# A two-layer diffusion transformer on one core: low halves of weights added by DMA, three more seven-product block pairs, and modulation work moved between tiles

## The chip, the cores and the metric

The kernel runs on one core of one Trainium2 chip, as a single launch. The core has five engines with queues of their own: TensorE (PE: matrix products into PSUM; its weight loads are listed apart as PEld), VectorE (DVE), ScalarE (ACT), GpSimd (POOL) and SyncE (SP), whose queue issues DMA transfers here. Within one queue the order is fixed when the program is built; between queues the work is ordered by semaphores. The metric is the time of one execution on the device in microseconds, as the median of several executions.

## The reference

Two layers, batch 1, 256 latent tokens and 256 context tokens, model width 1024, everything in float32. Each layer is a feed-forward block (SwiGLU, hidden width 2816), a mixer (a short convolution in layer 0, grouped-query attention in layer 1) and a second feed-forward block. Each of them is preceded by an RMS norm with a shift and a scale, and its result is gated; shifts, scales and gates ("modulation") come from a matrix product with the conditioning vector. The context stream is dropped after the attention. Cut to what matters:

```python
for i in range(DEPTH):                       # DEPTH = 2
    mod  = (silu(c)     @ mod_w[i] + mod_b[i]).reshape(bsz, 3, 3, 1, D_MODEL)
    modc = (silu(c_ctx) @ mod_w[i] + mod_b[i]).reshape(3, 3, D_MODEL)
    lat = lat + 0.5 * mod[:, 0, 2] * _swiglu(_modulate(lat, ...), ffn_w13[i, 0], ffn_w2[i, 0])
    cx  = cx  + 0.5 * modc[0, 2]   * _swiglu(_modulate(cx, ...),  ffn_w13[i, 0], ffn_w2[i, 0])
    h, hc = _modulate(lat, ...), _modulate(cx, ...)
    y, yc = _short_conv_mixer(...) if i == 0 else _gqa_mixer(...)
    lat = lat + mod[:, 1, 2] * y
    # context: the same, then its second feed-forward block, in layer 0 alone
    lat = lat + 0.5 * mod[:, 2, 2] * _swiglu(_modulate(lat, ...), ffn_w13[i, 1], ffn_w2[i, 1])

def _swiglu(h, w13, w2):
    gte, up = jnp.split(h @ w13, 2, axis=-1)
    return (silu(gte) * up) @ w2
```

## The kernel before

**Split products.** Activations stand transposed, features on partitions, the 512 tokens (latent, then context) along the free axis. [...] A product is three matmuls: high by high, high by low, low by high (`mm3`, lines 131 to 133; the third one, L133, is the one that reads the weights' low part). Splitting is `split` (L107): ScalarE writes the high part (L108), VectorE subtracts it from the source (L109).

**Loading weights.** `load_raw` (L102) issues a load on SP's queue into one of 8 buffers `wr`. The halves go to rings of 4 buffers `wh` and `wl` (`half`, L111), 1024 columns each. `load_w` (L117) loads and splits one block of 2048 columns.

**The feed-forward block** (`ffn`, L754). The 22 blocks of the hidden width go in thirds of 8, 7 and 7 (`THIRDS`). In each third the first product (`w13`) makes the gated hidden values of the third's blocks, then `project` (L569) multiplies them by the second weights (`w2a`, `w2b`), eight output tiles m = 0 to 7, and adds the result to the residual `x`. Both streams are computed together in layer 0 and in the first feed-forward block of layer 1 (`tot == T2`, 512 columns); the last one has the latent stream alone.

For 512 columns most blocks of the first product are done by `Pair` (L675): a two-by-two scheme with seven products instead of eight (7 products x 4 x 3 = 84 matmuls of 256 columns, against 48 matmuls of 512 for a block as it stands). It needs sums of the weights' quarters (`sums`, L696: VectorE), splits of them (`keep`), and a separate split of the quarter A22 into buffers `w4h` and `w4l` (L706 to L709, a ring of 2). A22 is used in a pair's last product (`four`, L749), which is run inside the following pair. The sums of the activations' quarters (T1 to T4) are made once for each block of the network. `AS_IS` (L25) lists the blocks of a first third that are done as they stand: 3 to 7 in the first feed-forward block, beside the blocks 0 to 2 of a start that is written out by hand.

**The second product** (`project`). Tiles m = 0, 1, 2 (two of them where no pair is left over) run side by side, with the last two products of the last pair between them; then one tile after the other, the last two split by stream if the projection ends the block (`late`). `ws2` (L847) loads and splits the weights of one tile; `get` (L586) asks for tiles up to two ahead. `finish` (L547) adds the gated result to `x`, and `tail` makes the sums of squares for the next norm.

**Modulation.** Apart from two chunks made by TensorE at the start, every modulation value is a dot product on VectorE: a unit (`mod_unit`, L167, tile `junk`) takes one 128x1024 tile of weights, and two units per stream pair share one load. The units are spread over the program by `tick(n)` (L210): each call owes n more units. `gate_of` (L233) makes sure that the whole chunk of a gate is done, and multiplies it by 0.5 where the reference does; `lazy_gate` (L865) calls it when the first tile needs it.

**Order.** The start is written out by hand (`FIRST_STEPS`), as is the attention; everywhere else a scheduler orders each engine's queue from the program's order and its own estimates. The convolution is in lines 1064 to 1101, the attention's output projection in line 1372; both output projections take their weights through `by_pairs` (L1103), two tiles in a pair of buffers.

Of the kernel before, what the change touches and what calls it, by code (L numbers as in the profile page):

```python
# [9 lines left out]
F32 = mybir.dt.float32  # L10
F32R = mybir.dt.float32r
BF16 = mybir.dt.bfloat16
AF = mybir.ActivationFunctionType
# [8 lines left out]
NM = 22  # L22
THIRDS = (8, 7, 7)

AS_IS = {(0, 0): range(3, 8), (0, 1): (), (1, 0): ()}  # L25

EARLY = 4
HEADS = 8
# [19 lines left out]
def hybrid_kernel(ctx: ExitStack, tc: tile.TileContext, a: dict, out: bass.AP):  # L48
# [58 lines left out]
    def split(hi, lo, src):  # L107
        nc.scalar.activation(out=hi, in_=src, func=AF.Copy)  # L108
        return nc.vector.tensor_tensor(out=lo, in0=src, in1=hi.bitcast(F32), op=ALU.subtract)  # L109

    def half():  # L111

        return tuple(
            wp.tile([P, 1024], F32R, name=nm(t), tag=t, bufs=4) for t in ("wh", "wl")
        )

    def load_w(src, n=2048, fine=False):  # L117
        raw = [load_raw(src[:, c : c + 1024]) for c in range(0, n, 1024)]
        hs = [half() for _ in raw]
        step = 512 if fine else 1024  # L120
        for c in range(0, n, step):
            hi, lo = hs[c // 1024]
            d = slice(c % 1024, c % 1024 + min(step, n - c))
            split(hi[:, d], lo[:, d], raw[c // 1024][:, d])
        return lambda o, w=P: tuple(t[:, o % 1024 : o % 1024 + w] for t in hs[o // 1024])

    def mm3(ps, w, m, first, last, more=False):
# [39 lines left out]
    def mod_unit(l, ch, pair, raw, j, v):  # L167

        mt = mod_tile(l, ch)
        kt = pair * 2 + j  # L170
        col = ch * KT + kt
        junk = mp.tile([P, D], BF16, name=nm("junk"), tag="junk", bufs=1)
        nc.vector.tensor_tensor_reduce(  # L173
            out=junk,
            in0=raw[j],
            in1=scbc[:, v, :],
            scale=1.0,
            scalar=modb[:, l, col : col + 1],
            op0=ALU.mult,
            op1=ALU.add,  # L180
            accum_out=mt[:, kt, v : v + 1],
        )
        done[l, ch] += 1
# [47 lines left out]
        return t  # L231

    def gate_of(l, j):  # L233
        m = mod_ready(l, 3 * j + 2)
        if j == 1:
            return m
        t = const.tile([P, KT, 2], F32, name=f"G{l}{j}", tag=f"G{l}{j}")
        nv = 1 if (l, j) == (1, 2) else 2
        nc.vector.tensor_scalar(
            out=t[:, :, :nv], in0=m[:, :, :nv], scalar1=0.5, scalar2=None, op0=ALU.mult  # L240
        )
        return t


    accs = {}
# [299 lines left out]
        return tail  # L545

    def finish(m, ps, c0, c1, gate, tail, wide=False):  # L547
        g = gate()
        for s in range(2):
            for o in [s * S - c0] if not wide else range(0, T2 if s == 0 else 0, S):  # L550
                if not c0 <= s * S < c1:
                    continue
                nc.vector.scalar_tensor_tensor(  # L553
                    out=x[:, m, s * S : s * S + S],
                    in0=ps[:, o : o + S],
                    scalar=g[:, m, s : s + 1],
                    in1=x[:, m, s * S : s * S + S],
                    op0=ALU.mult,
                    op1=ALU.add,
                )  # L560
        if tail:
            tail(m, c0, c1)
# [6 lines left out]
    def project(ws, src, nk, gate, tail, tot, late, ev, between=()):  # L569

        def products(ps, w, ks, c0, c1, wide=True):
            ms = [src(k, c0, c1) for k in ks]
            if wide and len(ms[0]) == 3:
                return mm_wide(ps, [w(k) for k in ks], ms, ks[0] == 0, ks[-1] == nk - 1)
            for k, m in zip(ks, ms):  # L580
                mm3(ps[:, : c1 - c0], w(k), m[:2], k == 0, k == nk - 1)

        nf = 3 if between else 2
        ahead = {}

        def get(m):  # L586
            for i in range(m, min(m + 3, KT)):
                if i not in ahead:
                    ahead[i] = ws(i)
            return ahead[m]  # L590

        w2 = [get(m) for m in range(nf)]
        p2 = [psum("py") for _ in range(nf)]
        cut = nk - 2 if between else nk - 1
        for i in range(nf):
            products(p2[i], w2[i], range(cut), 0, tot)
            if i < len(between):
                between[i]()
        if between:
            for i in range(nf):  # L600
                products(p2[i], w2[i], (nk - 2,), 0, tot)
        for i in range(nf):
            products(p2[i], w2[i], (nk - 1,), 0, tot)
            finish(i, p2[i], 0, tot, gate, tail, len(src(0, 0, tot)) == 3)
            tick(ev)

        for m in range(nf, KT - late):
            if tail and tot == S and m == KT - 2:
                ready()
            w = get(m)  # L610
            ps = psum("py")
            wide = len(src(0, 0, tot)) == 3 and m < KT - 1
            products(ps, w, range(nk), 0, tot, wide)
            finish(m, ps, 0, tot, gate, tail, wide)
            tick(ev)
        if late:

            wl = [get(m) for m in (6, 7)]
            if tail:
                ready()  # L620
            for s in range(2):
# [53 lines left out]
    class Pair:  # L675
# [4 lines left out]


        def __init__(self, src, h):
            self.h, self.w = h, {}
            self.raw = [load_raw(src[:, c : c + 1024]) for c in (0, 1024)]
            ts = half()
            for i, key in enumerate(("A11", "A12")):
                self.w[key] = [t[:, i * T2 : i * T2 + T2] for t in ts]
                split(*self.w[key], self.raw[i][:, T2:])
# [7 lines left out]
        def sums(self, n):  # L696
# [9 lines left out]
            self.w["A22"] = [  # L706
                wp.tile([P, T2], F32R, name=nm(t), tag=t, bufs=2) for t in ("w4h", "w4l")
            ]
            split(*self.w["A22"], r2[:, :T2])  # L709
            v = lambda t: t.rearrange("p (a c) -> p a c", a=2)  # L710
            tt(  # L711
                out=v(r2), in0=v(r2), in1=s2.unsqueeze(1).to_broadcast([P, 2, T2]),
# [38 lines left out]
            nc.vector.tensor_tensor(out=self.gm, in0=self.sg, in1=self.u, op=ALU.mult)  # L751
            split(g[0], g[1], self.gm)

    def ffn(l, b, h, tot, gate, tail, gs=(), ev=1.5, z=None):  # L754
        gs = list(gs)
        i0 = 0
        for t, n in enumerate(THIRDS):
            between = ()
            if tot == T2:
# [21 lines left out]
                prev = None  # L781
                for i in range(len(gs), n):
                    if t == 0 and not heads and i in AS_IS[l, b]:
                        w = load_w(a["w13"][l, b, i])
                        pp = psum("pg"), psum("pu")
                        if prev:
                            prev.seven()
# [8 lines left out]
                        w13_mm(pp, w, h, range(4, KT), 0, T2)  # L796
                        gs.append(new_pair("g"))
                        w13_post(pp, gs[-1], 0, T2)
                        tick(4)
                        continue  # L800
                    if heads:
                        pr = heads.pop(0)
# [44 lines left out]
            def ws2(m):  # L847
# [1 line left out]
                o = (m % 2) * n * P  # L849
                raw = load_raw(src[:, o : o + n * P], n * P)  # L850
                hi, lo = half()
                split(hi[:, : n * P], lo[:, : n * P], raw[:, : n * P])
                return lambda k: (hi[:, k * P : k * P + P], lo[:, k * P : k * P + P])

            cur = gs
# [2 lines left out]
                ws2,  # L858
                (lambda k, c0, c1: cur[k]) if tot == S
                else lambda k, c0, c1: (cur[k][0][:, c0:c1], cur[k][1][:, c0:c1]), n,  # L860
                gate, tail if end else None, tot, 2 if end and tot == T2 else 0, ev, between,
            )
            gs = []

    def lazy_gate(l, j):  # L865
        box = []

        def get():
            if not box:
                box.append(gate_of(l, j))  # L870
            return box[0]

        return get


    h = Plain()
# [170 lines left out]
    for i in range(3):  # L1047
        gs0.append(new_pair("g"))
        w13_post(pps[i], gs0[i], 0, T2)

    with tc.issue_after(rows["last"]):
        convk = cload("convk", [P, 3, KT])
        qg = cload("qg", [P, 1])
# [3 lines left out]


    hn = Plain()
    ffn(0, 0, h, T2, lazy_gate(0, 0), tail_norm(0, 1, hn), gs0, 2)  # L1060
    h = hn

    zs = []
    for m in range(KT):
# [4 lines left out]
        for c0, c1 in ((0, S), (S, T2)) if m == 0 else ((0, T2),):  # L1069
# [11 lines left out]
        u = tp.tile([P, T2], F32, name=nm("u"), tag="gm", bufs=3)  # L1081
        nc.vector.tensor_tensor(out=u, in0=xv, in1=pc, op=ALU.mult)
        d = tp.tile([P, T2], F32, name=nm("d"), tag="gm", bufs=3)
        nc.vector.tensor_scalar(
            out=d, in0=u, scalar1=convk[:, 1, m : m + 1], scalar2=None, op0=ALU.mult
        )
        u2 = u.rearrange("p (s t) -> p s t", s=2)
        d2 = d.rearrange("p (s t) -> p s t", s=2)
        nc.vector.scalar_tensor_tensor(
# [13 lines left out]
    def by_pairs(key, box=None):  # L1103
        box = box or {}

        def ws(m):
            if m // 2 not in box:
                box[m // 2] = load_w(a[key][m // 2])
            w = box[m // 2]
            return lambda k: w(k * 256 + (m % 2) * P)  # L1110

# [2 lines left out]
    hn = Blocks()  # L1114
    project(
        by_pairs("cw_out"), lambda k, c0, c1: (zs[k][0][:, c0:c1], zs[k][1][:, c0:c1]), KT,
        lazy_gate(0, 1), tail_norm(0, 2, hn), T2, 2, 1.5,
    )
    h = hn
    hn = Blocks()  # L1120
    ffn(0, 1, h, T2, lazy_gate(0, 2), tail_norm(1, 0, hn), (), 1.7)
    h = hn


    hn = Plain()
    ffn(1, 0, h, T2, lazy_gate(1, 0), tail_norm(1, 1, hn), (), 1.5)
    h = hn
    ap = ctx.enter_context(tc.tile_pool(name="ap", bufs=2))

# [210 lines left out]
    with tc.manual_schedule(engines={e.engine for e in (nc.tensor, nc.vector, nc.scalar, nc.gpsimd)}):  # L1340
# [29 lines left out]
    hn, hz = Beside(), Early()  # L1370
    roomy.append(True)
    project(
        by_pairs("wo", wos), lambda k, c0, c1: aos[k], KT, lazy_gate(1, 1), tail_early(1, 2, hn, hz), S, 0, 0,
    )
    ffn(
        1, 1, hn, S, lazy_gate(1, 2),
        lambda m, c0, c1: nc.sync.dma_start(out[m], x[:, m, :S]), z=hz,
    )

# [79 lines left out]
```

## Time and profile before

| what | value |
|---|---|
| median of 3 runs | 1569.32 us (1567.46 to 1571.04) |
| the profiled execution's own time | 1571.47 us |
| its span in the trace | 1569.7 us |
| granted TensorE clock | 0.998 |
| loads from SP and ACT (queues q1, q10) | 247 MB |
| low parts by VectorE, 128x1024 / 128x896 / 128x512 (A22) | 250 / 64 / 54 instructions |
| modulation units on VectorE | 224 |

The span is the stretch between the first and the last instruction that the profiler recorded. An engine's busy time is the time during which at least one of its instructions ran; a PE that is busy all the time can still be waiting a little, since the ends of its matmuls are modelled and overlap. The distance between the starts of two matmuls, and the list of waits, tell more than the busy share. In a row of a group, the last part (after the bar) is the busy time, the mean duration of one in ns, and the idle time of the engine ahead of them with its releaser.

### The profile page before, as it was taken

What the parts mean: (1) busy time and instruction counts of PE and PEld (TensorE: products, weight loads), DVE (VectorE), ACT (ScalarE), POOL (GpSimd) and SP (SyncE); (2) the same over time, 40 slices, a digit from 0 to 9 for tenths busy, and PEclk for the clock granted to TensorE, in tenths of its full rate; (3) what the DMA queues carried; (4) which work ended last, traced back from release to release, by engine and by line L of the source; (5) the groups of instructions that cost most, each with busy time, mean ns of one, the idle gap of its engine ahead of it and who ended that gap; (6) DMA issues with size and microseconds to landing.
All of it is one profiled execution on the core that took longest, in us unless ns stands there. A gap on an engine that the chain in (4) does not pass through costs nothing.

```text
span 1569.7 us, 25671 instructions
## 1 busy us (share of the span) xinstructions
PE 1557.7 (99%) x10210; PEld 1422.0 (91%) x10210; DVE 1333.4 (85%) x2129; ACT 733.8 (47%) x1213; POOL 25.4 (2%) x20
## 2 busy tenths in 40 slices
PE   9999999999999999999999999999999999999999
PEld 7888998999888899989899899999899889898888
DVE  5998789899997698978989989969978887887676
ACT  5622452545322365435345465435345445674553
POOL 0000000000000000000000000000000002300000
PEclk9999999999999999999999999999999999999999
DMA  9675246355565323542533614533733853366562
GB/s 373 224 237 180 89 132 187 107 173 159 194 209 166 114 75 108 177 146 87 189 126 117 196 41 135 187 108 118 239 112 114 265 154 106 123 207 221 171 199 75
DMA packets 72120, 248.80 MB, mean 159 GB/s; under 512 B 9024, under 2 KB 10816, under 8 KB 72000
## 3 DMA queue, kind: packets, MB, share of 16 engines
q1 hardware_dynamic: 69408, 245.40, 48.0%
q10 hardware_dynamic: 2592, 1.76, 0.4%
q8 instruction: 80, 1.31, 0.3%
q14 instruction: 40, 0.33, 0.1%
HBM read 244.77 MB, written 1.05 MB: 157 GB/s over the span
## 4 chain that ended last, share of the span: by engine, by line
PE 88%; DVE 6%; DMA 2%; ACT 2%; issue 1%; POOL 0%; POOLq 0%; SPq 0%; ACTq 0%; DVEq 0%
PE py L131 8%; PE py L132 8%; PE py L133 8%; PE p L131 6%; PE p L133 6%; PE p L132 6%; PE q L133 5%; PE q L131 4%; PE q L132 4%; PE py L139 2%; PE pu L139 2%; PE pg L139 2%; PE pg L132 1%; PE pg L133 1%; DMA wr<-in_w 1%; PE pu L132 1%
## 5 line engine op out<-in xcount | busy, mean ns | idle before, releaser
L108 ACT ACTIVATE wh<-wr 128x1024 fp32r<-128x1024 f32 (+2 forms) x442 | 393.7, 916 | 361.9 <-PE py L132 119.6
L109 DVE TENSOR_TENSOR wl<-wr,wh 128x1024 fp32r<-128x1024 f32 (+2 forms) x442 | 454.5, 1048 | 95.1 <-ACT wh L108 76.2
L173 DVE CUSTOM_DVE_ANT_0 junk<-wr,scbc,modb 128x1024 bf16<-128x1024 f32 x218 | 279.4, 1282 | 15.2 <-DMA wr<-in_modT 13.1
L131 PE MATMUL py<-gh,wh 128*128 128x512 f32 (+1 forms) x570 | 214.7, 377 | 0.0
L132 PE MATMUL py<-gl,wh 128*128 128x512 f32 (+1 forms) x570 | 214.0, 375 | 0.0
L133 PE MATMUL py<-gh,wl 128*128 128x512 f32 (+1 forms) x570 | 213.9, 375 | 0.0
L133 PEld LDWEIGHTS py<-gh,wl 128*128 128x128 f32 x570 | 108.3, 190 | 19.0
L131 PEld LDWEIGHTS py<-gh,wh 128*128 128x128 f32 x570 | 108.5, 190 | 18.4
L132 PEld LDWEIGHTS py<-gl,wh 128*128 128x128 f32 x570 | 108.5, 190 | 18.2
L131 PE MATMUL p<-th,wh 128*128 128x256 f32 x432 | 122.3, 283 | 0.0
L132 PE MATMUL p<-tl,wh 128*128 128x256 f32 x432 | 122.3, 283 | 0.0
L133 PE MATMUL p<-th,wl 128*128 128x256 f32 x432 | 122.2, 283 | 0.0
L553 DVE SCALAR_TENSOR_TENSOR x<-py,G,x 128x256 f32<-128x256 f32 x189 | 83.5, 479 | 36.3 <-PE py L133 25.1
L133 PE MATMUL q<-bh,wl 128*128 128x256 f32 x320 | 91.5, 286 | 0.1
L131 PE MATMUL q<-bh,wh 128*128 128x256 f32 x320 | 90.9, 284 | 0.4 <-ACT wh L108 0.4
L132 PE MATMUL q<-bl,wh 128*128 128x256 f32 x320 | 90.5, 283 | 0.0
L132 PEld LDWEIGHTS p<-tl,wh 128*128 128x128 f32 x432 | 82.8, 192 | 0.3
L131 PEld LDWEIGHTS p<-th,wh 128*128 128x128 f32 x432 | 82.8, 192 | 0.3
L133 PEld LDWEIGHTS p<-th,wl 128*128 128x128 f32 x432 | 82.8, 192 | 0.0
L108 ACT ACTIVATE w4h<-wr 128x512 fp32r<-128x512 f32 x54 | 33.8, 625 | 75.1 <-DMA wr<-in_w 56.9
L108 ACT ACTIVATE gh<-gm 128x512 fp32r<-128x512 f32 x66 | 41.6, 630 | 56.0 <-DVE gm L751 53.8
L711 DVE TENSOR_TENSOR wr<-wr,wr 128x1024 f32<-128x1024 f32 x54 | 66.0, 1222 | 0.7
(303 smaller groups left out, 3946.3 us busy)
## 6 DMA issues: line engine op xcount, KB each, us to landing
wr<-in_w SPq DMA_DIRECT2D x176, 512.0 KB, 4.5
wr<-in_modT SPq DMA_DIRECT2D x122, 512.0 KB, 4.5
wr<-in_w2b SPq DMA_DIRECT2D x64, 448.0 KB, 3.9
wr<-in_w2a SPq DMA_DIRECT2D x32, 512.0 KB, 4.7
pm<-in_mod SPq DMA_DIRECT2D x16, 512.0 KB, 10.2
wr<-in_cw_cx SPq DMA_DIRECT2D x16, 512.0 KB, 4.7
wr<-in_cw_b SPq DMA_DIRECT2D x8, 512.0 KB, 4.4
wr<-in_cw_out SPq DMA_DIRECT2D x8, 512.0 KB, 3.9
```

Of the source, the lines that this page charges most:

```text
L108: nc.scalar.activation(out=hi, in_=src, func=AF.Copy)
L109: return nc.vector.tensor_tensor(out=lo, in0=src, in1=hi.bitcast(F32), op=ALU.subtract)
L131: nc.tensor.matmul(ps, wh, mh, start=first, stop=False, **kw)
L132: nc.tensor.matmul(ps, wh, ml, start=False, stop=False, **kw)
L133: nc.tensor.matmul(ps, wl, mh, start=False, stop=last, **kw)
L139: nc.tensor.matmul(ps, w[0], m[2], start=first and n == 0, stop=False)
L173: nc.vector.tensor_tensor_reduce(out=junk, in0=raw[j], in1=scbc[:, v, :], scale=1.0, scalar=modb[:, l, col : col + 1], op0=ALU.mult, op1=A ...
L553: nc.vector.scalar_tensor_tensor(out=x[:, m, s * S : s * S + S], in0=ps[:, o : o + S], scalar=g[:, m, s : s + 1], in1=x[:, m, s * S : s * ...
L711: tt(out=v(r2), in0=v(r2), in1=s2.unsqueeze(1).to_broadcast([P, 2, T2]), op=ALU.subtract,)
```

## The change

Four things are edited.

1. A new function `split_far` makes a low part without VectorE: ScalarE writes the high part, then its negative into the low tile, and GpSimd issues a DMA that adds the weights from DRAM to it. It is used for A22 of every pair, for the second product's tiles m = 1 to 7 where both streams are computed, for block 4 of the first feed-forward block, and for the pairs of tiles 4/5 and 6/7 of the two output projections.
2. `AS_IS` is cut to blocks 3 and 4 in the first feed-forward block: blocks 5, 6 and 7 become pairs.
3. The gate is asked for tile by tile (`gate_of` returns a function of m that runs units only until the values of that tile exist), and the factor 0.5 moves from the gate into the units (`scale`) and into the bias (two VectorE operations at the end of the start).
4. The numbers of `tick` change. `project` no longer ticks behind its last tiles (6 and 7; 5, 6 and 7 where `late` is set), the first feed-forward blocks' ticks per tile rise, and the ticks between blocks done as they stand fall from 4 to 3. In the convolution, one product by a scalar moves from VectorE to ScalarE.

```diff
-AS_IS = {(0, 0): range(3, 8), (0, 1): (), (1, 0): ()}
+AS_IS = {(0, 0): range(3, 5), (0, 1): (), (1, 0): ()}
...
+    def split_far(hi, lo, raw, src):
+
+        nc.scalar.activation(out=hi, in_=raw, func=AF.Copy)
+        nc.scalar.activation(out=lo, in_=hi.bitcast(F32), func=AF.Copy, scale=-1.0)
+        nc.gpsimd.dma_start(out=lo, in_=src, accum_op=ALU.add)
...
-    def load_w(src, n=2048, fine=False):
+    def load_w(src, n=2048, fine=False, far=False):
...
-            split(hi[:, d], lo[:, d], raw[c // 1024][:, d])
+            ts = [t[:, d] for t in (hi, lo, raw[c // 1024])]
+            if far:
+                split_far(*ts, src[:, c : c + step])
+            else:
+                split(*ts)
...
-            scale=1.0,
+            scale=0.5 if ch in (2, 8) else 1.0,
...
     def gate_of(l, j):
-        m = mod_ready(l, 3 * j + 2)
...
+        ch = 3 * j + 2
+
+        def get(m):
+            while done.get((l, ch), 0) < (m // 2 + 1) * 2 * streams(l, ch):
+                next_unit()
+            return modv[l, ch]
+
+        return get
...
     def finish(m, ps, c0, c1, gate, tail, wide=False):
-        g = gate()
+        g = gate(m)
...
             finish(m, ps, 0, tot, gate, tail, wide)
-            tick(ev)
+            if m < (5 if late else 6):
+                tick(ev)
...
-            split(*self.w["A22"], r2[:, :T2])
+            split_far(*self.w["A22"], r2[:, :T2], self.src[:, 1024 : 1024 + T2])
...
-                        w = load_w(a["w13"][l, b, i])
+                        w = load_w(a["w13"][l, b, i], far=i > 3)
...
-                        tick(4)
+                        tick(3)
...
-                split(hi[:, : n * P], lo[:, : n * P], raw[:, : n * P])
+                ts = [t[:, : n * P] for t in (hi, lo, raw)]
+                if tot == T2 and m:
+                    split_far(*ts, src[:, o : o + n * P])
+                else:
+                    split(*ts)
...
-                gate, tail if end else None, tot, 2 if end and tot == T2 else 0, ev, between,
+                gate, tail if end else None, tot, 2 if end and tot == T2 else 0, ev[end], between,
...
+    for ch in (2, 8):
+        b = modb[:, :, ch * KT : ch * KT + KT]
+        nc.vector.tensor_scalar(out=b, in0=b, scalar1=0.5, scalar2=None, op0=ALU.mult)
...
-    ffn(0, 0, h, T2, lazy_gate(0, 0), tail_norm(0, 1, hn), gs0, 2)
+    ffn(0, 0, h, T2, gate_of(0, 0), tail_norm(0, 1, hn), gs0, (2.9, 2.4))
...
-        nc.vector.tensor_scalar(
-            out=d, in0=u, scalar1=convk[:, 1, m : m + 1], scalar2=None, op0=ALU.mult
-        )
+        nc.scalar.activation(out=d, in_=u, func=AF.Copy, scale=convk[:, 1, m : m + 1])
...
-                box[m // 2] = load_w(a[key][m // 2])
+                box[m // 2] = load_w(a[key][m // 2], far=m > 3)
...
-        lazy_gate(0, 1), tail_norm(0, 2, hn), T2, 2, 1.5,
+        gate_of(0, 1), tail_norm(0, 2, hn), T2, 2, 1.8,
...
-    ffn(0, 1, h, T2, lazy_gate(0, 2), tail_norm(1, 0, hn), (), 1.7)
+    ffn(0, 1, h, T2, gate_of(0, 2), tail_norm(1, 0, hn), (), (2.7, 2))
...
-    ffn(1, 0, h, T2, lazy_gate(1, 0), tail_norm(1, 1, hn), (), 1.5)
+    ffn(1, 0, h, T2, gate_of(1, 0), tail_norm(1, 1, hn), (), (2.5, 1.6))
```

In the pairs of values, the first is the number of units per tile in the projections of the first two thirds, the second in the last third.

More of the change, by code (lines that the diff above doesn't have):

```diff
@@ L233, in gate_of @@
     def gate_of(l, j):
-        m = mod_ready(l, 3 * j + 2)
[L235 to L238, printed above, removed]
-        nc.vector.tensor_scalar(
-            out=t[:, :, :nv], in0=m[:, :, :nv], scalar1=0.5, scalar2=None, op0=ALU.mult
-        )
-        return t
+        ch = 3 * j + 2
[4 more added lines that the diff above has]
+        return get
     accs = {}
@@ L682, in __init__ @@
         def __init__(self, src, h):
-            self.h, self.w = h, {}
+            self.h, self.w, self.src = h, {}, src
             self.raw = [load_raw(src[:, c : c + 1024]) for c in (0, 1024)]
@@ L752, in four, with ffn @@
             split(g[0], g[1], self.gm)
-    def ffn(l, b, h, tot, gate, tail, gs=(), ev=1.5, z=None):
+    def ffn(l, b, h, tot, gate, tail, gs=(), ev=(0, 0), z=None):
         gs = list(gs)
@@ L860, in ffn @@
                 else lambda k, c0, c1: (cur[k][0][:, c0:c1], cur[k][1][:, c0:c1]), n,
-                gate, tail if end else None, tot, 2 if end and tot == T2 else 0, ev, between,
+                gate, tail if end else None, tot, 2 if end and tot == T2 else 0, ev[end], between,
             )
             gs = []
[L865 to L873, printed above, removed]
     h = Plain()
@@ L1083, in hybrid_kernel @@
         d = tp.tile([P, T2], F32, name=nm("d"), tag="gm", bufs=3)
-        nc.vector.tensor_scalar(
-            out=d, in0=u, scalar1=convk[:, 1, m : m + 1], scalar2=None, op0=ALU.mult
-        )
+        nc.scalar.activation(out=d, in_=u, func=AF.Copy, scale=convk[:, 1, m : m + 1])
         u2 = u.rearrange("p (s t) -> p s t", s=2)
@@ L1372, in hybrid_kernel @@
     project(
-        by_pairs("wo", wos), lambda k, c0, c1: aos[k], KT, lazy_gate(1, 1), tail_early(1, 2, hn, hz), S, 0, 0,
+        by_pairs("wo", wos), lambda k, c0, c1: aos[k], KT, gate_of(1, 1), tail_early(1, 2, hn, hz), S, 0, 0,
     )
     ffn(
-        1, 1, hn, S, lazy_gate(1, 2),
+        1, 1, hn, S, gate_of(1, 2),
         lambda m, c0, c1: nc.sync.dma_start(out[m], x[:, m, :S]), z=hz,
```

## The prediction

> **What bounds the kernel now.** I read the page first, then TensorE's waits, then single stretches of the timeline.
>
> The busy times say that TensorE (PE) is the bound, VectorE (DVE) second, and that GpSimd (POOL) has almost nothing to do:
>
> ```profile
> PE 1557.7 (99%) x10210; PEld 1422.0 (91%) x10210; DVE 1333.4 (85%) x2129; ACT 733.8 (47%) x1213; POOL 25.4 (2%) x20
> ```
>
> A busy PE can hide short waits, so I looked at PE's own list of waits (engine, line, tile <- releaser: us in total, times, longest):
>
> ```profile
> PE ss L268 <- DVE acc L259: 1.5, 1, 1.5
> PE pg L132 <- DVE bl L109: 1.3, 2, 1.0
> ...
> PE q L131 <- ACT wh L108: 0.4, 1, 0.4
> ```
>
> The rest of that list (about 5 us) belongs to the start and to attention, which the change hardly touches. So whatever DVE is relieved of, PE can get back about 3 us by it. The first wait has a visible cause, in the chain of waits near 1250 us (start, length, what):
>
> ```profile
> 1251.56 5.22 DMA wr<-in_modT
> 1256.91 1.20 DVE junk L173
> 1258.21 0.35 DVE acc L259
> 1258.60 0.38 PE ss L268 x2
> ```
>
> A modulation unit (`junk`) stands in DVE's queue ahead of the last sum of squares and waits there for its own load.
>
> How long a PE instruction lasts is misleading, since matmuls overlap; what counts is from start to start. In the timeline, 512 columns step by 0.227 us and 256 columns by 0.120 us:
>
> ```profile
> 251.11 0.39 PE L133 MATMUL py<-gh,wl 128*128 128x512 f32 x1
> 251.34 0.39 PE L131 MATMUL py<-gh,wh 128*128 128x512 f32 x1
> 251.56 0.39 PE L132 MATMUL py<-gl,wh 128*128 128x512 f32 x1
> 251.57 0.19 PEld L133 LDWEIGHTS py<-gh,wl 128*128 128x128 f32 x1
> ...
> 251.79 0.39 PE L133 MATMUL py<-gh,wl 128*128 128x512 f32 x1
> ```
>
> ```profile
> 170.14 0.28 PE L132 MATMUL q<-hl,wh 128*128 128x256 f32 x1
> 170.26 0.28 PE L133 MATMUL q<-hh,wl 128*128 128x256 f32 x1
> ```
>
> **Three more block pairs.** A block as it stands has 48 products of 512 columns: 48 x 0.227 = 10.9 us. A pair of the seven-product scheme has 84 of 256: 84 x 0.120 = 10.1 us. Three of them (i = 5, 6, 7 of the first FFN) save 3 x 0.8 = 2.5 us of PE, which nothing can hide, since PE is the bound. On DVE a pair costs two 0.69 and two 1.22 us splits, 0.69 + 0.69 + 1.22 of sums, and 0.69 + 0.43 + 0.68 + 0.69 behind the products, 8.9 us; a block as it stands costs 2 x 1.22 + 0.69 + 0.69 = 3.8. That is 15 us more, in the stretch where DVE is full:
>
> ```profile
> 52.00:118.00 66.00, 66.00 (x293) 54.65 (x292) 65.21 (x97) 27.64 (x39) 0.00 (x0) 1.00 0.66 207
> ```
>
> (window: length, then busy PE, PEld, DVE, ACT, POOL). But the ticks there fall from 5 x 4 modulation units to 2 x 3 + 3 x 0.5, and 12.5 units x (1.28 + 0.08) = 17 us leave the stretch for the weaker ticks of later projections, now 2.9 instead of 2 a tile. It cancels; without that cover it would cost up to 15 us. I take 0.
>
> **The low parts.** Counted in the order of instructions, 130 low parts change hands: 57 A22 (128x512), 31 of 128x1024 and 42 of 128x896. For each, DVE's subtraction goes, ScalarE (ACT) writes the negated high part, and POOL issues a DMA that adds the weights from DRAM. The prices of the subtractions stand here (last: mean ns of one):
>
> ```profile
> L109 DVE TENSOR_TENSOR wl<-wr,wh 128x1024 fp32r<-128x1024 f32 x250 | 303.9, 1222 | 76.1 <-ACT wh L108 62.9 <-ACT sg L655 9.5 <-PE pu L141 3.1
> ...
> L109 DVE TENSOR_TENSOR wl<-wr,wh 128x896 fp32r<-128x896 f32 x64 | 68.8, 1086 | 8.5 <-PE pu L141 3.1 <-ACT wh L108 3.0 <-ACT sg L655 2.4
> ...
> L109 DVE TENSOR_TENSOR w4l<-wr,w4h 128x512 fp32r<-128x512 f32 x54 | 37.1, 687 | 1.2 <-ACT w4h L108 1.0
> ```
>
> DVE loses 54 x 0.69 + 31 x 1.22 + 42 x 1.09 = 121 us and the eight 0.48 us convolution products, and gains the 15: about 1224 busy. ACT gains 57 x 0.63 + 31 x 1.06 + 42 x 0.95 = 108 us, which lies in its idle time except where named below. The weights of these tiles are read from DRAM twice, 49 MB on top of 249; DMA is busy about half the time. On POOL's queue the DMAs stand in the order of ACT's negations, so none is held by one whose negation comes later; nothing else of POOL is near them. SP's queue no longer waits for a subtraction before it reuses these raw buffers, so loads only come earlier.
>
> What is worth PE time is when the new low part lands. For A22 the high part ends 17 to 19 us before its first reader, so any landing below 16 us is hidden. The far block of the first FFN has over 14 us, the output projection of the convolution 11.5 or more. The second product (`py`) is different. Its weights go through a ring of four `wh`/`wl` buffers; tiles m = 0, 1, 2 run side by side, and tile 4 can be split only when PE has finished tile 0, which leaves it PE's tile 3 and little else. In the second third of the first FFN:
>
> ```profile
> 245.19 2.64 ACT L108 ACTIVATE wh<-wr 128x896 fp32r<-128x896 f32 x3 [4.23 <-PE py L132]
> ```
>
> Those three are tiles 4, 5 and 6. In the changed order ACT runs high 4, high 5, negated 4: 245.19 + 2.64 = 247.83. PE loads the first low weights of tile 4 at 251.57 (above). So from issue to landing the adding DMA has 3.7 us, in all six thirds of 7 blocks (high part to reader is 5.6 us in each); with 8 blocks it is 6.2, which leaves 4.1, in three thirds. Everything of PE is queued behind that weight load, so what is late is lost whole. Tile 1 has about 5.5 us (high part 6.7 or more before the reader, less 0.95 and 0.2). In the attention output projection the second half of the third weight pair comes closest: high part to 1363.4, four small ACT operations to 1364.8, negation to 1365.8, reader at 1369.7: 3.9 us.
>
> No run shows an accumulating DMA. The nearest rows are plain loads of the same weights (448 KB, then 512 KB):
>
> ```profile
> DMA to landing us min/median/max: 3.2/3.9/6.0
> ```
>
> ```profile
> DMA to landing us min/median/max: 3.8/4.7/6.8
> ```
>
> Lower end: the fastest, 3.2 and 3.8, nothing late. Upper end: the slowest plus the issue on POOL, about 7 and 8. An adding DMA must also read what it adds to; at 373 GB/s, the fullest slice of the page, a second pass over the bytes is 1.2 or 1.4 us. I take the median plus half a pass, 4.5 and 5.4 us: 6 x 0.8 + 3 x 1.3 + 1.5 = 10.2 us lost.
>
> **Modulation off late tiles** takes the wait at 1258 us away and, with a lighter DVE, the two at `bl`: 1.5 + 1.3 = 2.8 us gained. At most it is 0; these are all the waits that it can reach. The gate product halved in advance is a few 0.17 us operations, hidden.
>
> **The sum.** -2.5 - 2.8 + 10.2 = +4.9. The profiled execution took 1571.47 us (span 1569.7 and 1.8 around it), so 1576.4 there; it lies 2.15 above the median of the three runs, 1569.32. On the median: **1574 us**.
>
> **Rivals.**
>
> *Hidden (faster).* If the adding DMA lands within 3.7 and 4.1 us, tile 4 is never late, and -2.5 - 2.8 = -5.3 remains: 1564 us. For it: the fastest plain loads, 3.2 and 3.8. Against it: their medians already miss, by 0.2 and 0.6. It decides from a median landing of 3.7 us down. [...]
>
> *Heavy.* If the adding path takes 7 us (POOL issues one after the other, and loads for the next blocks share the engines), tile 4 loses 3.3 x 6 + 2.9 x 3 = 28.5, tile 1 about 5 in all, attention 3: 1569.3 - 5.3 + 37 = 1601 us. For it: plain loads reach 6.0 and 6.8. Against it: half of them stay under 4.7.
>
> *Cancelled.* Landings near 4.0 and 4.7 cost 6 x 0.3 + 3 x 0.6 + 0.8 = 4.4 us, and the gain is eaten up: 1568 us.
>
> That the change does not do what it says is excluded by the order of instructions: the subtractions are gone, and PE has 3 x 36 more matmuls.
>
> **How the numbers follow.** About 0.2% (3 us) is what a measurement can tell from none. Forecast, 1572.5 to 1585: 0.42. Hidden, 1561 to 1566: 0.35. Heavy, above 1585: 0.15. Cancelled, within 3 us: 0.08. So faster 0.35, same 0.08, slower 0.57. The range of 8 in 10 takes in the hidden case and the heavy one: 1562 to 1601; the forecast's own range is 1572.5 to 1585.
>
> **What would show it.** Right: PE's list gains `py` L133 waiting for a DMA into `wl`, about nine times in the FFNs, 0.5 to 2 us each, always at the fifth tile of a projection; the wait near 1258 us is gone; DVE falls to about 1224, ACT rises to about 860. Wrong: no such wait and a PE span shorter by some 5 us (hidden); waits also at the second tile, or for `w4l` (heavy); or a DVE full between 52 and 118 us with PE waiting for its pair splits, which my zero for the three pairs denies.

## The result, and the profile after

| kernel | median | ratio to before, 95% interval |
|---|---|---|
| before | 1569.38 us (4 executions) | 1 |
| changed | 1695.60 us (1693.26 to 1699.54, 4 executions) | 1.0807 [1.0783, 1.0831] |

The change costs 126 us, 8.1%; the forecast was 1574 us, and the range ended at 1601. The profiled execution of the changed kernel took 1699.54 us (span 1697.8, granted clock 0.966 after 0.998).

The busy times of the changed kernel's page:

```profile
PE 1599.2 (94%) x10318; PEld 1453.8 (86%) x10318; DVE 1241.8 (73%) x2013; ACT 844.8 (50%) x1369; POOL 138.8 (8%) x150
```

VectorE lost 92 us of work, as intended, and TensorE has its 108 additional matmuls. But TensorE's share fell from 99 to 94%. Its list of waits in the changed kernel (in all, times, longest) says for what it stood:

```profile
PE py L143 <- DMA wl<-in_w2b: 39.5, 12, 6.8
PE py L143 <- DMA wl<-in_w2a: 29.4, 6, 7.3
PE ss L278 <- DVE acc L269: 5.5, 3, 3.1
PE py L143 <- DMA wl<-in_wo: 4.8, 2, 4.1
PE ss L278 <- ACT sq L261: 4.7, 2, 4.2
PE p L141 <- DVE p L756: 2.9, 1, 2.9
```

Before, no line of this list was above 1.5 us. Now 73.7 us stand behind the low parts of `wl` that a DMA adds. In the timeline, the 18 waits of the second product stand before tiles 1 and 4 of each of the nine projections with both streams, and nowhere else: 25 us at tile 1 (1.9 to 3.6 each), 44 us at tile 4 (2.9 to 7.3). No wait is behind `w4l`.

The same stretch that the prediction worked out (second third of the first feed-forward block, tile 4), in the timeline of the changed kernel:

```profile
262.38 1.80 ACT L113 ACTIVATE wh<-wr 128x896 fp32r<-128x896 f32 x2 [4.57 <-PE py L142]
264.08 1.78 ACT L114 ACTIVATE wl<-wh 128x896 fp32r<-128x896 f32 x2
...
265.42 1.79 POOL L115 DMA_DIRECT2D wl<-in_w2b  x2 [15.91 <-ACT wl L114]
...
268.75 0.39 PE L142 MATMUL py<-gl,wh 128*128 128x512 f32 x1
273.87 0.79 PE L143 MATMUL py<-gh,wl 128*128 128x512 f32 x1 [4.73 <-DMA wl<-in_w2b]
274.45 0.63 PE L141 MATMUL py<-gh,wh 128*128 128x512 f32 x1
274.88 0.63 PE L142 MATMUL py<-gl,wh 128*128 128x512 f32 x1
```

From issue (265.42) to need (268.98) there are 3.6 us; the transfer took 8.4. And the matmuls behind the wait step by 0.43 us, not by 0.227: TensorE got half its clock. The same place by windows (from:to and length, busy PE, PEld, DVE, ACT, POOL, then granted clock, DMA share, GB/s), changed kernel:

```profile
260.00:268.80 8.80, 8.80 (x41) 7.23 (x39) 6.30 (x14) 5.28 (x6) 2.50 (x3) 1.00 0.74 211
268.80:273.90 5.10, 0.37 (x3) 0.04 (x1) 3.89 (x7) 3.05 (x4) 0.15 (x1) 0.75 1.01 262
273.90:278.20 4.30, 4.30 (x10) 3.43 (x11) 2.30 (x4) 1.26 (x2) 1.48 (x2) 0.50 1.08 281
278.20:283.00 4.80, 4.80 (x22) 3.94 (x21) 3.37 (x7) 1.15 (x2) 1.14 (x2) 1.00 1.06 290
```

and in the kernel before, around its tile 4:

```profile
245.00:251.00 6.00, 6.00 (x28) 4.99 (x27) 5.82 (x11) 2.64 (x3) 0.00 (x0) 1.00 0.59 184
```

The reader is to see two things: 10 matmuls in 4.3 us where 22 fit in 4.8 us later, at a granted clock of 0.50; and a DMA share of 1, where it was 0.59: in this stretch the 16 engines are full. How long the transfers took is in the changed kernel's list of issues (KB each, median us to landing):

```profile
wr<-in_w2b SPq DMA_DIRECT2D x64, 448.0 KB, 4.1
wl<-in_w2b POOLq DMA_DIRECT2D x42, 448.0 KB, 9.5
w4l<-in_w POOLq DMA_DIRECT2D x57, 256.0 KB, 5.8
wl<-in_w2a POOLq DMA_DIRECT2D x21, 512.0 KB, 11.0
```

**Where 126 us went.** Over the trace from 60 us on, gaps of TensorE grew from 5 to 91 us. The windows at half clock add up to 116 us, of which 94 lie outside those gaps and cost half: 47 us, 3 before. The three pairs take 2.4 us of matmul time away, by the steps of the traces (3 x (48 x 0.227 - 84 x 0.120)). (91.2 - 5.5) + (46.9 - 3.4) - 2.4 = 126.8 us, beside 128.1 us of difference between the spans.

### The profile page after: what moved, and what is told of

Read it like the earlier page. It is cut to its first block, busy times and chain, and to the rows that moved or that the text cites. A ratio compares the mean times of both kernels' runs of the same rounds, so it can differ in the third digit from the quotient of the medians.

```text
span 1697.8 us, 26333 instructions
## 1 busy us (share of the span) xinstructions
PE 1599.2 (94%) x10318; PEld 1453.8 (86%) x10318; DVE 1241.8 (73%) x2013; ACT 844.8 (50%) x1369; POOL 138.8 (8%) x150
## 3 DMA queue, kind: packets, MB, share of 16 engines
q0 software_dynamic: 18720, 50.47, 16.0%
## 5 line engine op out<-in xcount | busy, mean ns | idle before, releaser
L108 ACT ACTIVATE wh<-wr 128x1024 fp32r<-128x1024 f32 (+2 forms) x375 | 324.7, 895 | 298.3 <-PE py L142 143.7
L109 DVE TENSOR_TENSOR wl<-wr,wh 128x1024 fp32r<-128x1024 f32 (+2 forms) x375 | 374.2, 1023 | 96.4 <-ACT wh L108 78.1
L143 PE MATMUL py<-gh,wl 128*128 128x512 f32 (+1 forms) x570 | 230.3, 404 | 68.9 <-DMA wl<-in_w2b 39.5
L141 PE MATMUL py<-gh,wh 128*128 128x512 f32 (+1 forms) x570 | 226.7, 398 | 0.0
L142 PE MATMUL py<-gl,wh 128*128 128x512 f32 (+1 forms) x570 | 226.5, 397 | 0.0
L143 PEld LDWEIGHTS py<-gh,wl 128*128 128x128 f32 x570 | 116.4, 204 | 98.0 <-DMA wl<-in_w2b 44.6
L563 DVE SCALAR_TENSOR_TENSOR x<-py,mod,x 128x256 f32<-128x256 f32 x213 | 93.5, 479 | 90.8 <-PE py L143 79.5
L141 PEld LDWEIGHTS py<-gh,wh 128*128 128x128 f32 x570 | 116.8, 205 | 20.2
L143 PE MATMUL p<-th,wl 128*128 128x256 f32 x456 | 129.0, 283 | 0.0
L115 POOL DMA_DIRECT2D w4l<-in_w x57 | 49.6, 876 | 749.4 <-ACT w4l L114 599.2
L713 DVE TENSOR_TENSOR wr<-wr,wr 128x512 f32<-128x512 f32 x57 | 39.2, 690 | 96.0 <-DMA wr<-in_w 91.3
L113 ACT ACTIVATE wh<-wr 128x896 fp32r<-128x896 f32 (+1 forms) x73 | 71.4, 990 | 47.2 <-PE py L142 33.0
L143 PE MATMUL q<-bh,wl 128*128 128x256 f32 x320 | 90.8, 284 | 0.6 <-DVE wl L109 0.6
L143 PEld LDWEIGHTS p<-th,wl 128*128 128x128 f32 x456 | 87.5, 192 | 0.0
## 6 DMA issues: line engine op xcount, KB each, us to landing
pm<-in_mod SPq DMA_DIRECT2D x16, 512.0 KB, 10.2
```

Of the source, the lines that this page charges most:

```text
L113: nc.scalar.activation(out=hi, in_=raw, func=AF.Copy)
L115: nc.gpsimd.dma_start(out=lo, in_=src, accum_op=ALU.add)
L141: nc.tensor.matmul(ps, wh, mh, start=first, stop=False, **kw)
L142: nc.tensor.matmul(ps, wh, ml, start=False, stop=False, **kw)
L143: nc.tensor.matmul(ps, wl, mh, start=False, stop=last, **kw)
L563: nc.vector.scalar_tensor_tensor(out=x[:, m, s * S : s * S + S], in0=ps[:, o : o + S], scalar=g[:, m, s : s + 1], in1=x[:, m, s * S : s * ...
```

## The experiments

**Which part is it?** Three kernels each keep a part. First, all of the change except the second product and the attention's projection, whose low parts VectorE makes again:

```diff
-                if tot == T2 and m:
+                if False:
...
-                box[m // 2] = load_w(a[key][m // 2], far=m > 3)
+                box[m // 2] = load_w(a[key][m // 2], far=m > 3 and key != "wo")
```

> The changed kernel, but the low parts of the second product and of the attention output projection are made by VectorE again; A22 by DMA, the three pairs and the moved modulation stay. Theory (the loss is the late landing of the adding DMA at tiles 1 and 4, 73.7 us of waits, plus the clock that halves after each, some 54 us): no wait of PE for a DMA into wl, granted clock 0.995 or more, 1562 to 1568 us. Rival (the moved modulation, the pairs or the A22 transfers cost the time): still above 1640 us, with PE waiting elsewhere.

Measured: 1580.47 us, ratio 1.0061 [1.0044, 1.0078]. 115 of the 126 us are gone, but not all: what is left is still slower than before. Second, the kernel before with the second product's DMA (`split_far` in `ws2` for m of 1 and more) and nothing else:

> The kernel before with one edit: low parts of the second product, tiles 1 to 7, by the adding DMA. Theory: the whole loss again, about 1569 + 74 + 50 = 1690 us, PE waiting for wl at tiles 1 and 4 of nine projections, clock about 0.97. Rival (the loss needs the other edits, for instance the A22 transfers on the same queue): less than half of it, under 1630 us.

Measured: 1684.66 us, ratio 1.0732 [1.0707, 1.0757]. The cost needs no other part of the change. Third, the kernel before with A22 alone by DMA:

> The kernel before with one edit: A22's low part by the adding DMA. Theory: landing near 6 us against 17 us of room, so hidden: 1566 to 1572 us, VectorE some 37 us less busy. [...]

Measured: 1575.55 us, ratio 1.0045 [1.0027, 1.0063]. No matmul waits for `w4l`, and yet 6.6 us are lost. Something other than the low part's own lateness costs time; this comes back below.

**Adding, or the way through GpSimd?** The changed kernel with the second product's transfers as plain copies from the same queue:

```diff
+        if add:
             nc.gpsimd.dma_start(out=lo, in_=src, accum_op=ALU.add)
+        else:
+            nc.gpsimd.dma_start(out=lo, in_=src)
...
+                    split_far(*ts, src[:, o : o + n * P], add=False)
```

> The changed kernel with the second product's DMAs copying instead of adding, so its low parts are the whole weights: the addition is left out. If the addition is what makes landing slow (9.5 us for 448 KB), landing falls to about 4.5 us and the time to 1570 to 1590 us. If it is the path through GpSimd, landing stays above 8 us and the time above 1670 us.

Measured: 1648.94 us (one execution), between the two expectations. Its list of issues:

```profile
wl<-in_w2b POOLq DMA_DIRECT2D x42, 448.0 KB, 7.8
...
wl<-in_w2a POOLq DMA_DIRECT2D x21, 512.0 KB, 8.3
```

Of the 9.5 us of an adding transfer, 4.1 are those of a plain load on SP's queue, 3.7 more come with GpSimd's queue and the loads that share the engines with it (this run does not tell these two apart), and 1.7 with the addition. In time, by this one execution, adding is 47 of the 126 us.

**Is the half clock a cost of its own?** The changed kernel with matmuls that keep TensorE working where it would wait, 13 of 512 columns ahead of tile 1 and 20 ahead of tile 4 of each second product with both streams:

```diff
+        def fill(ps, n):
+            if tot == T2 and between:
+                mv = src(0, 0, tot)[0]
+                for _ in range(n):
+                    nc.tensor.matmul(ps[:, :tot], w2[0](0)[0], mv, start=True, stop=True)
...
+            if i == 1:
+                fill(p2[i], 13)
...
+            if m == 4:
+                fill(ps, 20)
```

> [...] Theory 'the wait and the half clock behind it are two costs': the waits stay hidden under the added matmuls, the granted clock goes from 0.966 to above 0.985, and 30 to 50 of the 126 us come back: 1645 to 1668 us. Rival 'the half clock only stretches work that would have waited for the next transfer anyway': the clock rises, but the waits at tile 4 grow by as much, and the time stays at 1680 us or more.

Measured: 1711.25 us, ratio 1.0898 [1.0873, 1.0923], clock 0.983. The theory's time missed. The rival's (1680 us or more) came, but not by its mechanism, since the waits at tile 4 shrank instead of growing. The waits for `wl` from `w2b` fell from 39.5 to 3.6 us, and the half clock's cost from 47 to 23 us. But other waits came up in the list of this kernel:

```profile
PE py L141 <- ACT gh L108: 15.0, 5, 4.5
PE ss L278 <- DVE acc L269: 12.9, 4, 6.7
...
PE py L143 <- DMA wl<-in_w2b: 3.6, 3, 1.6
```

All gaps together still make 57 us, and the added matmuls 67 (297 steps of 0.227). So the wait and the half clock do fall separately, but the low part is not the only thing that is late; how far the added matmuls themselves bring on the new waits is not shown.

**Read the low part later.** The changed kernel with all products of the high part first, so that a tile's low part is first read behind 14 or 16 matmuls instead of two (an estimate from the step of 0.227 us: 2.7 or 3.2 us later, less in the tiles that start side by side):

```diff
+            if tot == T2 and nk < 9:
+                po = ps[:, : c1 - c0]
+                for k, m in zip(ks, ms):
+                    nc.tensor.matmul(po, w(k)[0], m[0], start=k == 0, stop=False)
+                    nc.tensor.matmul(po, w(k)[0], m[1], start=False, stop=False)
+                for k, m in zip(ks, ms):
+                    nc.tensor.matmul(po, w(k)[1], m[0], start=False, stop=k == nk - 1)
+                return
```

> The changed kernel with the products of a second-product tile in another order: all products with the weights' high part first, those with the low part last. [...] Theory 'each transfer is late by the 2.3 to 7.7 us that the waits show': the waits fall from 74 us to about 28, about ten of eighteen are left, the half clock falls in step, and the time is 1605 to 1640 us. Rival 'the software queue cannot keep up in the long run': the waits move to the tiles behind (2, 5, 6), and the time stays above 1670 us.

Measured: 1672.88 us, ratio 1.0654 [1.0624, 1.0684]: 23 us better than the change. That is the rival's number, but not its mechanism: of the 16 waits that are left, 14 still stand at tiles 1 and 4, and those at tiles 5 and 6 are 0.7 us each. Its waits:

```profile
PE py L596 <- DMA wl<-in_w2b: 17.7, 10, 5.5
PE py L596 <- DMA wl<-in_w2a: 15.1, 6, 4.9
PE ss L278 <- DVE acc L269: 9.5, 4, 3.9
PE py L593 <- ACT gh L108: 7.2, 3, 4.2
PE q L141 <- ACT gm L753: 6.4, 2, 6.1
```

The direct waits are halved, as expected (32.8 us of 68.9). What fell short is the rest: again TensorE waits for ScalarE and VectorE, at the norms and in the pairs.

**Is the issue held up?** In the changed kernel GpSimd's issue sometimes came long after the negation (28.6 us in 7 waits with no visible releaser). The changed kernel with `dynamic_dma_scratch_size` at 3072 instead of 1024:

> [...] Rival 'the transfers themselves queue at the DMA engines': landings counted from the negation stay the same, the time stays at 1688 to 1702 us.

Measured: 1690.66 us, ratio 1.0767 [1.0734, 1.0800]. Counted over the 63 second-product transfers, the longest time from negation to issue fell from 9.1 to 0.6 us; from the start of the high part to landing the median is 13.0 us, 13.2 in the changed kernel. The issue was held, and it mattered little (5 us): released earlier, the transfers land hardly earlier.

**The pairs alone**, in the kernel before:

```diff
-AS_IS = {(0, 0): range(3, 8), (0, 1): (), (1, 0): ()}
+AS_IS = {(0, 0): range(3, 5), (0, 1): (), (1, 0): ()}
```

> The kernel before with three more block pairs in the first feed-forward block (blocks 5, 6 and 7) and nothing else: every low part by VectorE, modulation where it was. [...] Rival 'VectorE pays': the pairs' sums and splits, some 4.4 us of VectorE work per block more, fall in the stretch where the kernel before has VectorE busiest, TensorE waits for it and drops its clock: 1572 to 1580 us, and it is this that keeps the version with VectorE's low parts (1580.5 us) above the kernel before.

Measured: 1571.58 us, ratio 1.0007 [0.9996, 1.0019]: no difference that the measurement can tell. By the steps of the traces (0.227 and 0.120 us) the pairs' matmuls take 2.4 us less. The fastest of 12 executions gained 1.1 us (1566.85 against 1567.97, both at clock 1.000), and 8 of the 12 ran at 0.998 or 0.997, where 13 of 17 of the kernel before ran at 0.999 or 1.000: the rest of the gain seems to go into short waits (TensorE's gaps in the profiled execution sum to 9 us, 5 before) and the clock behind them.

**The modulation edits alone**, every low part by VectorE and no new pair:

> The kernel before with the edits of the modulation alone (gates asked for tile by tile, 0.5 in the units, new ticks, none behind the last tiles, one product of the convolution on ScalarE); every low part by VectorE, no new pair. Theory 'the last tiles are freed' (the prediction's step, 2.8 us): 1565 to 1568 us. Rival 'the sums of the next pair take their place': without modulation units VectorE's queue has, ahead of the last tile's addition to x, a sum that waits for a load, as it has in the version without the second product's transfers, where TensorE waits 4.0 us at the end of the convolution's output projection and then runs 6.8 us at half clock: 7.4 us for it, less the waits that are gone, 1572 to 1578 us.

Measured: 1574.43 us, ratio 1.0033 [1.0022, 1.0044], slower by 5.7 us, the rival's number. But its mechanism is not in this trace: there is no wait at the end of the convolution's projection, and the wait at the norm near 1260 us is still there, longer than before (first line of its list):

```profile
PE ss L276 <- DVE acc L267: 3.5, 3, 2.0
```

2.1 us are there in the fastest executions at full clock (1569.66 against 1567.54), the rest goes with the clock (0.997 or 0.998 in most). What costs the 2.1 us stays open. **Pairs and modulation together**, every low part by VectorE (`split_far` calls `split`):

> The changed kernel with every low part by VectorE: the three pairs and the modulation edits stay, no transfer by GpSimd. Theory 'A22 alone costs 6.6 us, the rest of 1580.5 us is of the other edits': 1571 to 1577 us. Rival 'only all the edits together fit VectorE, which now has 64 + 57 more splits': VectorE's busy time returns to 1340 us or more, waits come back at the norms, 1578 us or more. If it falls below 1568 us it beats the kernel before.

Measured: 1574.82 us, ratio 1.0031 [1.0019, 1.0043]. VectorE's busy time is 1344.0 us, as the rival said, but the time is the theory's. Against the first experiment (1580.47 us), which has the transfers of A22, of block 4 and of the convolution's projection besides, it is 5.7 us faster: the price of transfers that no product waits for shows a second time. By its median, no version run here beats the kernel before.

The blocked queue that the rival of the modulation run named does exist where A22 goes by DMA too. In the timeline of the kernel with VectorE's second product:

```profile
555.70 0.69 DVE L713 TENSOR_TENSOR wr<-wr,wr 128x512 f32<-128x512 f32 x1 [2.83 <-DMA wr<-in_w]
556.31 0.48 DVE L563 SCALAR_TENSOR_TENSOR x<-py,mod,x 128x256 f32<-128x256 f32 x1
556.88 0.42 ACT L261 ACTIVATE sq<-x 128x256 f32<-128x256 f32 x1 [4.47 <-DVE x L563]
```

A sum of the next pair waits in VectorE's queue for its load; behind it stands the last addition to `x`, then the square, then TensorE (4.0 us).

**The transfer where there is time.** The changed kernel with the second product's DMA only for four tiles that never waited:

```diff
-                if tot == T2 and m:
+                if tot == T2 and m in (2, 3, 6, 7):
...
-                box[m // 2] = load_w(a[key][m // 2], far=m > 3)
+                box[m // 2] = load_w(a[key][m // 2], far=m > 3 and key != "wo")
```

> The changed kernel with the transfer only for tiles 2, 3, 6 and 7 of the second product; tiles 1, 4 and 5 and the attention's output projection by VectorE. The waits of the changed kernel stood before tiles 1 and 4 alone. Theory 'only those two tiles are too early for a landing 13 us behind the high part': 1578 to 1590 us. Rival 'each transfer also delays the plain loads beside it, for which VectorE's queue then waits' (91 us behind wr<-in_w in the changed kernel, 13 us before): 36 transfers are left of 63, so some half of the loss stays, 1610 us or more.

Measured: 1605.67 us, ratio 1.0227 [1.0201, 1.0253], between the two. TensorE waits 6.9 us for `wl` of the second product, nearly all of it twice at tile 7 (3.0 and 3.8 us), which waits in no projection of the changed kernel. But its gaps sum to 32 us (5 in the kernel before). The timeline shows one of the others, from cause to effect:

```profile
1252.44 0.08 DVE L183 DVE_READ_ACCUMULATOR2_ANT mod<- 128x1 f32 x1
1256.95 1.28 DVE L183 CUSTOM_DVE_ANT_0 junk<-wr,scbc,modb 128x1024 bf16<-128x1024 f32 x1 [4.42 <-DMA wr<-in_modT]
1258.16 0.08 DVE L183 DVE_READ_ACCUMULATOR2_ANT mod<- 128x1 f32 x1
1258.16 0.43 DVE L756 TENSOR_TENSOR p<-p,gm 128x256 f32<-128x256 f32 x1
...
1258.64 0.58 PE L141 MATMUL p<-th,w4h 128*128 128x256 f32 x1 [3.70 <-DVE p L756]
```

The modulation unit's plain load was issued at 1245.88 and landed at 1256.81: 10.9 us, beside an adding transfer (1246.16 to 1256.33) and other plain loads on the same engines. VectorE stood 4.42 us for it, the pair's sum stood behind the unit, and TensorE behind that sum. This is the second cost: late plain loads that block VectorE's queue. In the kernel before, VectorE's list of waits has

```profile
DVE junk L173 <- DMA wr<-in_modT: 13.1, 15, 2.4
DVE wr L702 <- DMA wr<-in_w: 12.6, 13, 1.9
```

and in the changed kernel

```profile
DVE wr L713 <- DMA wr<-in_w: 91.3, 33, 6.9
...
DVE junk L183 <- DMA wr<-in_modT: 66.0, 48, 4.6
```

The kernel with A22 alone by DMA has 27.9 us (`wr`) and 25.9 us (`junk`). Counted over the trace of the changed kernel (from 60 us on), 249 plain loads that overlapped a transfer of GpSimd landed in 6.2 us median, 104 of them above 7 us; the 194 others in 4.1 us, 2 of them above 7. In the kernel before it is 4.4 us, and 3 of 443.

**The second cost by itself.** The kernel before, every low part by VectorE, with adding transfers into a tile that is never read:

```diff
+        g = go[:, len(made) : len(made) + 1]
+        made.append(g)
+        nc.scalar.activation(out=g, in_=hi.bitcast(F32)[:, :1], func=AF.Copy)
+        nc.gpsimd.tensor_copy(out=unread[:, :1], in_=g)
+        for c in (0, n - 448):
+            nc.gpsimd.dma_start(out=unread, in_=src[:, c : c + 448], accum_op=ALU.add)
...
+                if tot == T2 and m:
+                    again(hi, src[:, o : o + n * P], n * P)
```

> The kernel before, every low part by VectorE, and besides it the transfers alone: for each of the 63 second-product tiles that the change takes by DMA, GpSimd issues two adding transfers of 224 KB of its weights into a tile that nobody reads, once the tile's high part is written (each pair waits for the one before it, so that they are more spread out than in the changed kernel). Theory 'an adding transfer also costs by delaying the plain loads beside it' (249 plain loads that overlapped one landed in 6.2 us median in the changed kernel, 104 of them over 7 us; without one 4.1 us, 2 of 194): loads over 7 us and waits of VectorE for loads grow here too, and the time is 1578 to 1600 us. Rival 'only the direct wait for the low part costs': 1567 to 1573 us.

Measured: 1583.54 us, ratio 1.0097 [1.0072, 1.0122]. The traffic alone costs 13 us, though no product ever waits for it. (Each pair of transfers also brings a ScalarE instruction of one column, whose part in this is not told apart.) In VectorE's waits of the profiled execution, the fastest of the four (1578.27 us):

```profile
DVE wr L716 <- DMA wr<-in_w: 32.7, 24, 3.5
```

32.7 us where the kernel before has 12.6. Loads above 7 us are few here (8 of 248 that overlap), in keeping with transfers that are more spread out (each pair waited for the one before it); so 13 us is more likely too little than too much for the denser traffic of the change.

## Why the prediction was wrong, step by step

- **The direction was right, the mechanism half right.** The wait `py` L133 (now L143) on a DMA into `wl` came, and the budget at tile 4 was right where it was worked out: 3.7 us forecast, 3.6 in the trace. Nine waits were forecast there, and nine came, but of 2.9 to 7.3 us instead of 0.5 to 2: 44 us in all, where the sum had 8.7. The attention's output projection waits 4.8 us, where the sum had 1.5.
- **The step that failed: the price of the adding DMA**, "the median plus half a pass, 4.5 and 5.4 us", with "about 7 and 8" as upper end. Measured: 9.5 and 11.0 us median, 14.9 at most; even the upper end lay below the median. The nearest rows were plain loads on SP's queue, and they say nothing of GpSimd's queue (a plain copy through it: 7.8 and 8.3 us) and of the addition (1.7 and 2.7 more, where half a pass was 0.6 and 0.7). "DMA is busy about half the time" hid the rest: the transfers come in bursts, and in the burst the share is 1 (1.01 to 1.08 in the windows above).
- With that price tile 1, with "about 5.5 us", is late too: nine more waits, 25 us. This is what the *Heavy* rival said would show it; its 7 us was still too little, and its 1601 us had no clock in it. It also counts tile 1 low: 1.5 us over the room, nine times, is 13.5 us and not "about 5", so by its own price it comes to some 1610 us.
- **A term was missing from the sum: the clock behind a wait.** "What is late is lost whole" is too little here: behind the waits TensorE ran at half clock, which cost 47 us, over half of what the gaps themselves cost. With the waits that I forecast, up to 2 us, the clock would mostly have stayed up (over ten traces, half clock behind 4 of 35 gaps of TensorE of 0.8 to 1.5 us and 9 of 22 of 1.5 to 2.2 us); it is the size of the wait that brings in the second loss (15 of 26 of 2.2 to 3 us, all 62 of 3 us or more).
- **"So loads only come earlier" was wrong.** SP's queue may issue earlier, but the loads land later beside the transfers (6.2 us against 4.1), VectorE stands in its queue for them, and an edit that frees VectorE gives TensorE nothing. Traffic alone costs 13 us, in the more spread-out form that was run. A22, which I had as hidden since 16 us of room were there, costs 6.6 us with no wait for it. VectorE's waits for loads doubled there (from 26 to 54 us); that these make the 6.6 us is the likely reading, and no run isolates it.
- **Three pairs, -2.5 us "which nothing can hide":** the matmuls fell by as much (2.4 us by the steps of the trace), the time by nothing that can be measured (-0.6 to +3 us). What failed is "which nothing can hide".
- **Cover on VectorE in the first feed-forward block, 0:** no wait of TensorE appears between 48 and 118 us of the changed kernel; it stands. (The 15 us more of VectorE counts the three A22 splits, which go by DMA; 13 is right, and it changes nothing.)
- **Modulation, -2.8 us:** +5.7 us when alone. The wait near 1258 us did not go: 1.5 us before, 2.0 with the modulation edits alone. Why is open.
- **Loads of the engines:** VectorE 1241.8 us against 1224 forecast, ScalarE 844.8 against 860; the weights that are read twice make 50.5 MB, 49 forecast.
- ***Hidden*:** a landing of 3.7 us or less was its condition, and the fastest of the 63 adding transfers took 5.3 (448 KB: 9.5 median). Even plain copies in their place took 3.7 at best and 7.8 median for 448 KB.

## What to carry to other kernels

Price a transfer by rows of the same queue, kind and traffic (here 448 KB landed in 4.1 us as a plain load on SP's queue and in 9.5 as an adding transfer on GpSimd's); where there are none, take the upper end from a burst in which the DMA engines are full, not from the mean share. Moving work from a nearly full engine to DMA was not free here (13 us for the traffic alone), where VectorE's queue also waits for loads: ask which loads will share the engines, and what stands behind the instruction that waits for them. And when TensorE is the bound, price a wait of some 3 us or more with the slow clock behind it, by this case about half as much again (47 us behind 91 us of gaps).

## What the runs showed of the hardware

- **The clock follows the length of the wait.** Over ten traces (before, after, and the experiments up to the pairs alone), from 20 us on: all 62 gaps of TensorE of 3 us or more were followed, within 3 us of their end, by a stretch at half clock (3.4 us, 6.8 us in most cases from 4 us on, sometimes 10.2); of 2.2 to 3 us, 15 of 26; of 1.5 to 2.2 us, 9 of 22; of 0.8 to 1.5 us, 4 of 35. Matmuls of 512 columns then step by 0.43 us instead of 0.227. The scatter between executions of the kernel before goes with the clock as well: 1567 to 1569 us at a mean clock of 1.000, 1574 at 0.996.
- **Adding transfers occupy the DMA engines longer.** From the queue's share of the engines' time, less that of the kernel whose second product and attention projection are VectorE's (16.0% of 1697.8 us less 7.0% of 1573.1 us, times 16 engines, over 18720 - 9072 packets): 268 ns a packet. With copies in place of the second product's additions (12.5% of 1647.2 us): 159 ns.
- **GpSimd's issues came late at the smaller `dynamic_dma_scratch_size`**: at 1024, an issue came up to 9.1 us behind its negation; at 3072, within 0.6.
- **Plain loads beside such transfers landed later**: in the changed kernel those that overlapped one took 6.2 us median and up to 15.9, the others 4.1 median.
